# First attention of a two-layer hybrid transformer on one core: the conditioning-vector steps start at item 10, one to every second item, and ScalarE multiplies for the latent stream

## The chip, the cores and the metric

One core of a Trainium2 chip runs the whole program in one launch. The metric is device time in microseconds. TensorE (PE in the rows; PEld is its weight loading), VectorE (DVE), ScalarE (ACT), GpSimd (POOL) and SyncE (SP) each work through a queue of their own in order; the first four compute, SP here starts the DMAs.

## The reference, cut to what matters

Two layers run over 512 latent tokens and 256 context tokens of width 1024; the first uses grouped-query attention, the second latent attention, and each is followed by a squared-ReLU MLP. Every sub-layer is modulated by six vectors (shift, scale, gate, twice) that are linear maps of the conditioning input, one set per stream:

```python
mod_lat = (silu_c @ w_ada[i] + b_ada[i])[:, None, :]
mod_ctx = silu_cc @ w_ada[i] + b_ada[i]
sh_a, sc_a, g_a, sh_m, sc_m, g_m = jnp.split(mod_lat, 6, axis=-1)
...
x = layer_norm(alpha * x + g_a * y_lat, ln_g[i, 0], ln_b[i, 0])
```

In the first attention, latent queries attend in one softmax to 256 context and 512 latent keys, context queries to the context keys alone, with 16 query heads of width 64.

## The kernel before, in words

The first attention works through 8 pairs of heads. A pair has five rounds: first half of the latent queries tile 0, the context round, tile 1, then the two tiles of the second half; 40 rounds in all, here numbered r0 to r39 (r1, r6, r11 ... are context rounds). In a round PE computes the scores of both heads of the pair (lines 852 and 853, for context 843 and 844), DVE takes the negated row maximum (`nm`, line 690; 693 for context), ACT the exponentials (`prob`, line 691; 695 for context). In the next round PE transposes these (line 707), ACT and DVE copy them out (`pT` or `pC`, lines 710 and 712), and later PE multiplies them with the values (line 731), after which `rb` (723), a transpose (740), `rinv` (742) and `o` (743) divide by the row sums. Scores have two buffers (`big`), so the scores of a head wait until the exponentials of the same head in the round before have been read. The query split for the next pair (`QS`, two casts on ACT by line 62, each followed by a subtraction on DVE by line 65) stands in two of the five rounds.

Work that the attention does not need rides along. `fill` is called twice a round, once for each item i (so 80 items), and issues a step of a conditioning vector when its argument is true. There are 32 steps: two vectors (v = 2, 3) in two halves, 8 steps each. A step loads 128x512 of the weight (`araw`, two buffers, a DMA on SP), multiplies it by one column of the conditioning input for each of the two streams (line 204 on POOL or 206 on ACT; stream 0 is the latent one and goes into `atmp`, one buffer; stream 1 overwrites `araw`), and adds both to accumulators on POOL (`aacc`, line 208). The first step of a half writes the accumulators directly. Six items after the eighth step PE sums the accumulators (line 215). At given items the split of the output projection's weights is placed too: `wh` (ACT, line 62, 128x1024) and `wl` (DVE, line 65).

PE's order is written by hand. The order on ACT, DVE, POOL and SP comes from a scheduler that places instructions by its own idea of when they can run, so an instruction may stand far ahead of the place where the program issues it.

Of the kernel before, what the change touches and what calls it, by code (L numbers as in the profile page):

```python
# [39 lines left out]
def backbone(ctx, tc, a, out):  # L40
# [14 lines left out]
    def big():  # L55
        return ps.tile([P, 2, 512], F32, name="big", tag="big", bufs=2)

    def one():
        return ps.tile([P, 512], F32, name="one", tag="one", bufs=4)
# [75 lines left out]
    def vec_bias(layer, v, half, n):  # L135
        w = D // n
        return ada_bias(a["b_ada"][layer, v, half * w : half * w + w].rearrange("(g c) -> g c", g=4), w // 4)

    def ada_finish(layer, v, half, n, o, bias):

        w = D // n
        q = w // 4
        row = ada_row(o[:, 0:q], bias)
        if v % 3 == 2:
            for g in range(4):
                c0 = half * w + g * q
                nc.sync.dma_start(gates[2 * layer + v // 3, :, c0 : c0 + q], row[32 * g : 32 * g + 2, :])
            return
        tp = o[:, 256 : 256 + q]
        m = q // P  # L150
        for c in range(m):
            nc.tensor.transpose(tp[:, c * P : (c + 1) * P], row[:, c * P : (c + 1) * P], ident)
        if (layer, v) not in modT:
            modT[layer, v] = const.tile([P, KD, 2], F32, name=f"modT{layer}{v}")
        mv = modT[layer, v].rearrange("p (n g j) s -> p n j g s", n=n, g=4)
        for s in range(2):
            nc.vector.tensor_copy(
                out=mv[:, half, :, :, s], in_=tp.rearrange("p (c g r) -> p c g r", c=m, g=4)[:, :, :, s]
            )
# [17 lines left out]
    def ada_vec(layer, v, half, n, streams, pools, mult):  # L177

        w = D // n
        rawp, tmpp, accp = pools
        accs, bias = {}, []
        src = a["w_ada"][layer, v]

        def step(k):
            if k == 0:
                bias.append(vec_bias(layer, v, half, n))
            t = rawp(src[k, :, half * w : half * w + w])  # L190
            for s in streams:
                eng = mult(k, s)
                sc = scT[:, k, s : s + 1]
                if k == 0:
                    accs[s] = dst = accp(s)
                elif eng == "dve":
                    nc.vector.scalar_tensor_tensor(
                        out=accs[s], in0=t, scalar=sc, in1=accs[s], op0=ALU.mult, op1=ALU.add
                    )
                    continue  # L200
                else:
                    dst = t if s == streams[-1] else tmpp()
                if eng == "pool":
                    nc.gpsimd.tensor_tensor(out=dst, in0=t, in1=sc.to_broadcast([P, w]), op=ALU.mult)
                else:
                    nc.scalar.activation(dst, t, AF.Identity, scale=sc)  # L206
                if k > 0:
                    nc.gpsimd.tensor_tensor(out=accs[s], in0=accs[s], in1=dst, op=ALU.add)  # L208

        def end():  # L210
            o = one()
            q = w // 4
            for g in range(4):
                for i, s in enumerate(streams):
                    nc.tensor.matmul(
                        o[32 * g : 32 * g + 32, 0:q], onehot[:, 1 - s : 33 - s], accs[s][:, g * q : g * q + q],
                        start=(i == 0), stop=(i == len(streams) - 1),
                    )
            ada_finish(layer, v, half, n, o, bias[0])

        return [lambda k=k: step(k) for k in range(KD - 1)] + [lambda: (step(KD - 1), end)[1]]
# [278 lines left out]
    def ada_raw(src):  # L500
# [4 lines left out]
    ada_pools = (  # L505
        ada_raw, lambda: adp.tile([P, 512], F32, name="atmp", tag="atmp"),
        lambda s: adp.tile([P, 512], F32, name="aacc", tag="aacc", bufs=4),
    )
    phase = ["act"]
    steps = []  # L510
    for v in (2, 3):
        for h in range(2):
            steps += ada_vec(0, v, h, 2, (0, 1), ada_pools, lambda k, s: phase[0])
    fill = Fill(steps, 6)
    qp = pool(st_qkv, "qp")
    rope = raw_tile(a["rope_gqa"].rearrange("p a t d -> p (a t d)"), 512)[:, 0:512]
# [156 lines left out]
    class Attn:  # L673
# [78 lines left out]
        def run(self, first, prep, scores, vcol, o_of, npair, ctx_scores, fill, at):  # L752

            rounds = []
            for p in range(npair):
                rounds += [(p, 0, 0)] + ([(p, None, 0)] if ctx_scores is not None else [])  # L760
                rounds += [(p, 0, 1), (p, 1, 0), (p, 1, 1)]
            state, PT, sums = {0: first}, {}, {}
            av, steps, last = [], [], []
            n = 0

            def score(p, hf, q, h):
                S = big()
                if (p, hf) not in sums:
                    sums[p, hf] = self.ap.tile([P, 2, 2], F32, name="sm", tag="sm", bufs=4)
                if hf is None:  # L770
                    ctx_scores(state[p], h, S)
                    return self.softmax(S, 2, CTX, sums[p, hf][:, :, h])
                scores(state[p], h, NCT + hf * 2 + q, S)
                return self.softmax(S, 1, 384, sums[p, hf][:, q, h : h + 1])

            def turn(p, hf, q, pts):
                if hf is None:
                    PT[p, hf] = t = self.ap.tile([P, 2, NCT, 2, P], F32, name="pC", tag="pC")
                    self.transposed(pts, t.rearrange("p t n h c -> p (t n) h c"), 1)
                    return  # L780
                if q == 0:
                    PT[p, hf] = self.ap.tile([P, 2, NT, 2, P], F32, name="pT", tag="pT", bufs=2)
                self.transposed(pts, PT[p, hf][:, q], self.nact)

            with tc.manual_schedule(engines={nc.tensor.engine}):
                while rounds or last or av:
                    now = []
                    if rounds:
                        p, hf, q = rounds.pop(0)
                        if hf == 0 and q == 0 and p + 1 < npair:  # L790
                            state[p + 1], steps = prep(p + 1)
                        now = [(p, hf, q, [score(p, hf, q, h) for h in range(2)])]
                    ready = av[:1]
                    for it in last:
                        turn(*it)
                    if steps:
                        steps.pop(0)()
                    for f, end in ready:
                        f()
                        if end:  # L800
                            end()
                    av = av[1:]
                    if last and (last[0][1] is None or last[0][2] == 1):
                        p, hf = last[0][:2]
                        lo = 0 if hf is None else NCT + hf * 2
                        av += self.values(
                            PT[p, hf], sums[p, hf],
                            lambda kt, hh, p=p: vcol(kt, 2 * p + hh), range(NCT if hf is None else NT),
                            o_of(p)[:, lo : lo + 2, :],
                        )  # L810
                    last = now
                    for i in (n, n + 1):
                        if fill is not None:
                            fill(i % 5 < 2)
                        for f in at.get(i, []):
                            f()
                    n += 2
                if fill is not None:
                    fill.rest()
# [688 lines left out]
```

## Time and profile before

| | |
|---|---|
| median of 3 runs | 1685.24 us (1681.62 to 1685.29) |
| profiled execution | 1686.92 us, its span 1685.1 us |
| PE busy in the span | 1625.9 us (96%) |
| DVE, ACT, POOL busy | 1117.6, 721.7, 444.0 us |
| first attention | 129 to 332 us of the span |

The profile's span leaves out 1.8 us around it. Busy shares are over the whole program; the stage in question is about an eighth of it.

### The profile page before, as it was taken

The numbers are of one execution on the slowest core, as the hardware profiler recorded it, in microseconds if no ns is written. First come the engines' busy times: TensorE is split into PE (matmuls) and PEld (weight loads), VectorE is DVE, ScalarE is ACT, GpSimd is POOL, SyncE is SP. The second block draws the span as 40 slices with busy tenths as digits, with TensorE's granted clock in tenths as the row PEclk, the third lists the DMA queues.
The fourth block names the chain that finished last, engine by engine and source line by source line (L and its number), as shares of the span: only waits on it lengthen the run. The fifth ranks groups of instructions, "written<-read, shape, count | busy, mean of one in ns | idle before, by whom it ended". The sixth has DMA issues, their size and how long they took to land.

```text
span 1685.1 us, 23746 instructions
## 1 busy us (share of the span) xinstructions
PE 1625.9 (96%) x9266; PEld 1366.8 (81%) x9266; DVE 1117.6 (66%) x1700; ACT 721.7 (43%) x1317; POOL 444.0 (26%) x317
## 2 busy tenths in 40 slices
PE   7998999999999999999999999999999999999996
PEld 6875777778888888898889898888878888888884
DVE  4778888777856667555547666766658655555587
ACT  3324676634643344333112356666653522222221
POOL 0247888034323245223000321000004200000034
PEclk9998999999999999999999999999999999999998
DMA  8413113132434356344213122001022433332222
GB/s 324 137 52 106 51 57 101 58 119 100 164 123 138 105 190 196 123 137 151 75 51 109 61 95 91 1 1 38 26 99 102 164 100 100 100 100 91 97 75 76
DMA packets 51969, 172.05 MB, mean 102 GB/s; under 512 B 6776, under 2 KB 6928, under 8 KB 51856
## 3 DMA queue, kind: packets, MB, share of 16 engines
q1 hardware_dynamic: 51824, 170.51, 30.3%
q8 instruction: 73, 1.20, 0.3%
q14 instruction: 40, 0.33, 0.1%
q10 hardware_dynamic: 32, 0.02, 0.0%
HBM read 161.03 MB, written 9.47 MB: 101 GB/s over the span
## 4 chain that ended last, share of the span: by engine, by line
PE 80%; DVE 10%; ACT 3%; DMA 3%; POOL 2%; issue 2%; DVEq 0%; SPq 0%; ACTq 0%; POOLq 0%
PE one L89 10%; PE one L91 10%; PE one L90 10%; PE big L978 7%; PE big L981 7%; PE big L982 7%; PE one L731 6%; PE one L707 4%; PE one L914 2%; PE one L915 2%; PE one L918 2%; DVE wl L65 2%; POOL xr L208 1%; PE big L1359 1%; PE big L852 1%
## 5 line engine op out<-in xcount | busy, mean ns | idle before, releaser
L62 ACT CAST wh<-raw 128x1024 fp32r<-128x1024 f32 (+3 forms) x172 | 171.9, 1016 | 404.6 <-PE one L91 210.8
L65 DVE TENSOR_TENSOR wl<-raw,wh 128x1024 fp32r<-128x1024 f32 (+3 forms) x172 | 218.6, 1284 | 175.0 <-ACT wh L62 173.8
L978 PE MATMUL big<-actH,wh 128*128 128x384 f32 (+2 forms) x800 | 280.7, 352 | 1.3 <-ACT wh L62 1.3
L981 PE MATMUL big<-actL,wh 128*128 128x384 f32 (+2 forms) x800 | 279.9, 350 | 0.4 <-DVE actL L65 0.3
L982 PE MATMUL big<-actH,wl 128*128 128x384 f32 (+2 forms) x800 | 279.5, 350 | 0.0
L89 PE MATMUL one<-wh,hh 128*128 128x512 f32 x640 | 256.1, 401 | 9.4 <-ACT hh L62 4.4
L91 PE MATMUL one<-wh,hl 128*128 128x512 f32 x640 | 253.9, 398 | 2.8 <-DVE hl L65 2.8
L90 PE MATMUL one<-wl,hh 128*128 128x512 f32 x640 | 255.1, 399 | 1.3 <-DVE wl L65 1.3
L1062 DVE TENSOR_TENSOR yacc<-yacc,one 128x512 f32<-128x512 f32 x260 | 174.4, 682 | 113.5 <-PE one L91 113.2
L208 POOL TENSOR_TENSOR xr<-xr,raw 128x1024 f32<-128x1024 f32 x49 | 129.0, 2633 | 249.2 <-ACT raw L206 247.8
L978 PEld LDWEIGHTS big<-actH,wh 128*128 128x128 f32 x800 | 150.2, 188 | 15.0 <-ACT wh L62 2.1
L981 PEld LDWEIGHTS big<-actL,wh 128*128 128x128 f32 x800 | 150.3, 188 | 13.4 <-DVE actL L65 1.1
L982 PEld LDWEIGHTS big<-actH,wl 128*128 128x128 f32 x800 | 150.1, 188 | 12.6 <-issue 0.4
L89 PEld LDWEIGHTS one<-wh,hh 128*128 128x128 f32 x640 | 121.7, 190 | 41.1 <-ACT hh L62 5.1
L91 PEld LDWEIGHTS one<-wh,hl 128*128 128x128 f32 x640 | 121.2, 189 | 32.0 <-DVE hl L65 3.2
L90 PEld LDWEIGHTS one<-wl,hh 128*128 128x128 f32 x640 | 121.8, 190 | 27.5 <-DVE wl L65 1.7
L691 ACT ACTIVATE prob<-big,nm 128x768 f32<-128x768 f32 x128 | 115.9, 908 | 56.0 <-DVE nm L690 55.8
L690 DVE TENSOR_REDUCE nm<-big 128x1 f32<-128x768 f32 x128 | 119.6, 953 | 14.7 <-PE big L1363 8.6
L707 PE MATMUL one<-ident,prob 128*128 128x128 f32 x832 | 104.1, 274 | 1.7 <-ACT pT L710 1.7
L731 PE MATMUL one<-pT,V 128*64 128x256 f32 x768 | 98.7, 393 | 2.6 <-DVE pT L712 2.6
L707 PEld LDWEIGHTS one<-ident,prob 128*128 128x128 f32 x832 | 95.6, 142 | 5.2 <-ACT pT L710 2.2
L328 POOL TENSOR_TENSOR xr<-xr,ln_g 128x1024 f32<-128x1024 f32 x8 | 20.9, 2617 | 265.4 <-PE one L915 242.8
(246 smaller groups left out, 2844.4 us busy)
## 6 DMA issues: line engine op xcount, KB each, us to landing
raw<-in_mlp_w_dram SPq DMA_DIRECT2D x128, 512.0 KB
raw<-in_w_ada_dram SPq DMA_DIRECT2D x56, 512.0 KB
sraw<-in_w_ada_dram SPq DMA_DIRECT2D x16, 512.0 KB
araw<-in_w_ada_dram SPq DMA_DIRECT2D x32, 256.0 KB
raw<-in_w_o_dram SPq DMA_DIRECT2D x16, 512.0 KB
xr<-xres SPq DMA_DIRECT2D x14, 512.0 KB
raw<-in_w_qkv_dram SPq DMA_DIRECT2D x12, 512.0 KB
ada<-in_w_ada_dram SPq DMA_DIRECT2D x8, 512.0 KB
```

The lines of the kernel that those rows point to most:

```text
L62: return nc.scalar.copy(out=dst, in_=src)
L65: return nc.vector.tensor_tensor(out=dst, in0=src, in1=hi.bitcast(F32), op=ALU.subtract)
L89: nc.tensor.matmul(o, lh, rh, start=start, stop=False)
L90: nc.tensor.matmul(o, lh, rl, start=False, stop=False)
L91: nc.tensor.matmul(o, ll, rh, start=False, stop=stop)
L208: nc.gpsimd.tensor_tensor(out=accs[s], in0=accs[s], in1=dst, op=ALU.add)
L707: nc.tensor.transpose(tp[:, j * P : (j + 1) * P], pts[j % 2][:, k * P : (k + 1) * P], ident)
L731: nc.tensor.matmul(acc[64 * hh : 64 * hh + 64, 0:256], v(kts[n], hh), PT[:, :, n, hh, :], start=(n == 0), stop=(n == len(kts) - 1),)
L978: mm = nc.tensor.matmul(o, wh[:, ks], aH[:, k, s:e], start=(k == 0), stop=False)
L981: nc.tensor.matmul(o, wh[:, ks], aL[:, k, s:e], start=False, stop=False)
L982: nc.tensor.matmul(o, wl[:, ks], aH[:, k, s:e], start=False, stop=(k == KD - 1))
L1062: nc.vector.tensor_tensor(out=yacc[i][:, cs], in0=yacc[i][:, cs], in1=accs[hf], op=ALU.add)
```

## The change

The first product of the two streams moves from POOL to ACT in all 32 steps, and the items at which a step is issued change from two of every five, from item 0 on, to every second one from item 10 on.

```diff
-            steps += ada_vec(0, v, h, 2, (0, 1), ada_pools, lambda k, s: phase[0])
+            steps += ada_vec(0, v, h, 2, (0, 1), ada_pools, lambda k, s: phase[0] if s else "act")
...
-                            fill(i % 5 < 2)
+                            fill(i >= 10 and i % 2 == 0)
```

`phase[0]` is "pool" by the time these steps run. The call of `fill` in the second attention is the same line with other work (`fill` may be None there), and the steps' DMAs, adds and final PE sums are the same in number.

How the change moves instructions is seen in the built programs. First POOL, in the middle of a half, before: one step is the run from one `atmp` product to the next.

```order
L204 TENSOR_TENSOR atmp_1800<-araw_1798,scT_75 128x512
L208 TENSOR_TENSOR aacc_1494<-aacc_1494,araw_1791 128x512
L208 TENSOR_TENSOR aacc_1492<-aacc_1492,atmp_1800 128x512
L204 TENSOR_TENSOR araw_1798<-araw_1798,scT_75 128x512
L204 TENSOR_TENSOR atmp_1908<-araw_1906,scT_75 128x512
L208 TENSOR_TENSOR aacc_1494<-aacc_1494,araw_1798 128x512
```

After, POOL in the first half of a vector, around its third and fourth step:

```order
L208 TENSOR_TENSOR aacc_1766<-aacc_1766,atmp_1880 128x512
L204 TENSOR_TENSOR araw_1878<-araw_1878,scT_75 128x512
L208 TENSOR_TENSOR aacc_1768<-aacc_1768,araw_1878 128x512
L208 TENSOR_TENSOR aacc_1766<-aacc_1766,atmp_1937 128x512
L204 TENSOR_TENSOR araw_1935<-araw_1935,scT_75 128x512
L208 TENSOR_TENSOR aacc_1768<-aacc_1768,araw_1935 128x512
```

Four instructions of a step became three, and the add of `atmp` now waits for ACT; before, the next step's `atmp` product stood ahead of the add that frees `araw`, and now it no longer does.

ACT in round r17 (first the copy `pC` and the exponentials of both heads), before:

```order
L62 CAST QS_2318<-one_2429 64x384 x2
L710 COPY pC_2465<-one_2466 128x512
L691 ACTIVATE prob_2453,sm_2320<-big_2447,nm_2452 128x768
L691 ACTIVATE prob_2462,sm_2320<-big_2456,nm_2461 128x768
L742 COPY rinv_2486<-one_2437 128x256
L723 COPY rb_2536<-sm_2390 128x256
```

The same round of ACT after:

```order
L691 ACTIVATE prob_2439,sm_2291<-big_2433,nm_2438 128x768
L710 COPY pC_2451<-one_2452 128x512
L206 ACTIVATE atmp_2847<-araw_2845,scT_75 128x512
L62 CAST wh_2852<-raw_2658 128x1024
L691 ACTIVATE prob_2448,sm_2291<-big_2442,nm_2447 128x768
L742 COPY rinv_2472<-one_2416 128x256
L206 ACTIVATE atmp_2905<-araw_2903,scT_75 128x512
```

A product and a weight cast now stand between the exponentials of the two heads; this cast stood in round r23 before. The 32 products of line 206 stand on ACT from the stage ahead of the attention (two of them) and from r2 to r29, although the program issues them from r5 to r36.

DVE in the context round r31, before (`nm` of the two heads, a weight split, the copies `pT`):

```order
L693 TENSOR_REDUCE nm_3301<-big_3296 128x2
L65 TENSOR_TENSOR wl_3282<-raw_3095,wh_3281 128x1024
L712 COPY pT_3306<-one_3313 128x512
L65 TENSOR_TENSOR QS_3205<-one_3243,QS_3205 64x384
L712 COPY pT_3306<-one_3319 128x512
```

And after:

```order
L693 TENSOR_REDUCE nm_3291<-big_3285 128x2
L743 TENSOR_TENSOR o5_3087<-one_3195,rinv_3269 128x256
L65 TENSOR_TENSOR wl_3282<-raw_3095,wh_3281 128x1024
L693 TENSOR_REDUCE nm_3301<-big_3296 128x2
L712 COPY pT_3306<-one_3313 128x512
L712 COPY pT_3306<-one_3319 128x512
```

The weight split stands between the two maxima instead of behind both, and the query split no longer stands between the two copies.

## Rows read from the trace of the kernel before

**Rows 1.** The page's first line.

```profile
span 1685.1 us, 23746 instructions
```

**Rows 2.** Windows: busy PE, PEld, DVE, ACT, POOL; granted clock, DMA share, GB/s.

```profile
129.00:168.00 39.00, 31.14 (x219) 22.13 (x218) 32.84 (x60) 18.48 (x43) 30.64 (x26) 0.87 0.28 96
168.00:257.00 89.00, 87.48 (x684) 69.93 (x685) 72.39 (x117) 62.50 (x154) 77.30 (x68) 1.00 0.18 56
281.00:290.00 9.00, 6.53 (x56) 4.44 (x55) 7.67 (x12) 5.53 (x16) 8.84 (x7) 0.83 0.27 80
```

**Rows 3.** Groups of POOL, 129 to 332 us: busy, mean ns, idle before.

```profile
L208 POOL TENSOR_TENSOR aacc<-aacc,araw 128x512 f32<-128x512 f32 x28 | 36.8, 1315 | 0.2
...
L204 POOL TENSOR_TENSOR atmp<-araw,scT 128x512 f32<-128x512 f32 x28 | 29.2, 1043 | 17.4 <-DMA araw<-in_w_ada_dram 17.1 <-POOL araw L204 0.2
```

**Rows 4.** Timeline of POOL in one step: start, us, instruction, idle before.

```profile
169.24 1.28 POOL L208 TENSOR_TENSOR aacc<-aacc,araw 128x512 f32<-128x512 f32 x1
...
173.36 1.04 POOL L204 TENSOR_TENSOR atmp<-araw,scT 128x512 f32<-128x512 f32 x1 [0.61 <-DMA araw<-in_w_ada_dram]
```

**Rows 5.** Groups of ACT, 129 to 332 us.

```profile
L710 ACT COPY pT<-one 128x512 f32<-128x512 f32 x32 | 18.7, 584 | 16.5 <-PE one L707 16.5
...
L62 ACT CAST wh<-raw 128x1024 fp32r<-128x1024 f32 x6 | 6.3, 1052 | 0.0
```

**Rows 6.** Line 206 elsewhere in the program: ns min/median/max.

```profile
L206 ACT ACTIVATE raw<-raw,scT x49: 1144/1153/1157, 433.6 to 792.7; 128x1024 f32<-128x1024 f32 x49
```

**Rows 7.** Timeline of ACT in r17.

```profile
219.37 0.59 ACT L710 COPY pC<-one 128x512 f32<-128x512 f32 x1 [0.51 <-PE one L707]
219.85 0.91 ACT L691 ACTIVATE prob<-big,nm 128x768 f32<-128x768 f32 x1
...
220.74 0.90 ACT L691 ACTIVATE prob<-big,nm 128x768 f32<-128x768 f32 x1
```

**Rows 8.** Timeline of PE: second head's scores of r18.

```profile
222.11 0.34 PE L852 MATMUL big<-KL,QS 128*128 128x384 f32 x1
```

**Rows 9.** Timeline of ACT: the second head's exponentials of r2.

```profile
147.29 0.89 ACT L691 ACTIVATE prob<-big,nm 128x768 f32<-128x768 f32 x1
```

**Rows 10.** Timeline of PE: second head's scores of r3.

```profile
148.32 0.45 PE L852 MATMUL big<-KL,QS 128*128 128x384 f32 x1
```

**Rows 11.** Timeline of ACT in r15 and r16: the query split and rinv.

```profile
212.75 0.47 ACT L62 CAST QS<-one 64x384 fp32r<-64x384 f32 x1 [0.62 <-DVE QS L65]
213.36 0.37 ACT L742 COPY rinv<-one 128x256 f32<-128x256 f32 x1
```

**Rows 12.** Timeline of ACT around r27.

```profile
264.34 0.47 ACT L62 CAST QS<-one 64x384 fp32r<-64x384 f32 x1 [1.37 <-DVE QS L65]
265.85 0.59 ACT L710 COPY pC<-one 128x512 f32<-128x512 f32 x1 [1.03 <-PE one L707]
...
269.94 0.59 ACT L710 COPY pT<-one 128x512 f32<-128x512 f32 x1 [0.47 <-PE one L707]
```

**Rows 13.** Timeline of PE: r5 after its stall, r6, and r31.

```profile
164.01 0.89 PE L610 MATMUL one<-ident,q 128*128 128x128 f32 x3 [2.43 <-ACT pT L710]
164.83 2.81 PE L731 MATMUL one<-pT,V 128*64 128x256 f32 x12
...
174.43 1.52 PE L731 MATMUL one<-pT,V 128*64 128x256 f32 x12
...
286.21 2.15 PE L731 MATMUL one<-pT,V 128*64 128x256 f32 x12 [1.29 <-DVE pT L712]
```

**Rows 14.** Timeline of DVE in r5, r31, and r34.

```profile
160.39 1.20 DVE L252 TENSOR_TENSOR modB<-modA,lnbT 128x16 f32<-128x16 f32 x1
...
283.41 2.15 DVE L65 TENSOR_TENSOR wl<-raw,wh 128x1024 fp32r<-128x1024 f32 x1
...
286.19 0.56 DVE L65 TENSOR_TENSOR QS<-one,QS 64x384 fp32r<-64x384 f32 x1
...
301.15 1.22 DVE L65 TENSOR_TENSOR wl<-raw,wh 128x1024 fp32r<-128x1024 f32 x1
```

## The prediction, on record before the changed kernel ran

> **What bounds the kernel now.** I read the page first, then busy time by stretch, then the groups of ACT and POOL in the attention, then timelines of the rounds in which PE waits. The profiled execution has a span of 1685.1 us [rows 1] and took 1686.92 us in all, 0.1% above the median of 1685.24, so the sum below is made on its span and added to the median. 0.3% of that median is 5.1 us, about what a measurement of this kernel can tell from no change.
>
> The attention has two kinds of stretch [rows 2]. From 168 to 257 us PE is busy 87.48 of 89 us at a granted clock of 1.00: PE is the bound, and ACT with 62.50 us has 26.5 us free, DVE 16.6. From 129 to 168 PE is busy only 31.14 of 39 us, at 0.87, and from 281 to 290 only 6.53 of 9 us, at 0.83. In both, POOL is busy almost throughout (30.64 and 8.84 us). So the change can win in the second kind and lose in the first.
>
> POOL before spends about 1.04 us on a product and 1.32 us on an add of `araw` [rows 3], some 4.7 us a step, and waits 17.4 us for `araw` in all. One turn of its loop shows why: the add that frees `araw` ends at 170.52 (169.24 + 1.28), and the product that waits for the new `araw` starts at 173.36 [rows 4]. That is 2.84 us from a buffer set free to its next use, and the product stands ahead of the next add, so a step took 5.1 us. The steps thus ran from 140 to 298 us, and the old argument of `fill` did not pace them; nor need the new one.
>
> **The change part by part.** It takes 32 products of 1.04 us off POOL, 33 us. A step is then product, two adds: about 3.7 us. That is work on an engine for which PE does not wait in rounds, so it counts only through DVE (below). The DMAs are the same 32.
>
> On ACT it adds 32 products of 128x512. ACT's copies cost 0.584 us at 512 columns and 1.052 at 1024 [rows 5], 0.47 less for half the columns. The trace has line 206 at 128x1024 alone, 1.153 us [rows 6], so I estimate 1.153 - 0.47 = 0.69 us; the bounds are 0.58 (the copy) and 1.15 (the long product). Consecutive instructions overlap: the copy at 219.37 lasts 0.59 us and the next starts at 219.85 [rows 7], so 0.11 comes off, and a product holds the queue for 0.58, say 0.6 us. The total of 19 us fits the idle time of ACT. What matters is where each one stands, because the order moves: a product between the two exponentials of a round delays the second, and with it the second head's scores a round later on PE.
>
> How much room is there? In r17 the second exponentials end at 221.64 (220.74 + 0.90), and the scores that need their buffer start at 222.11 [rows 7, 8]: 0.47 us. In r2 they end at 148.18 [rows 9] and the scores of r3 follow at 148.32 [rows 10], where PE waits for them; so 0.14 of a gap is the least, and the room of a steady round is 0.33 us.
>
> Term 1, r2: a product stands between the two exponentials, where there is no room: +0.6 us. It could be given back if DVE were late in r5 anyway (bounds 0 and 0.6); I take all of it.
>
> Term 2, the query split. In r15 its second cast waits 0.62 us for DVE, and `rinv` follows it [rows 11]. After, `rinv` (0.37 us) stands between the two casts in r6, r11 and r21, in r6 with a product as well. Where `rinv` is ready early it fits the 0.62 us, where its input from PE is late the cast waits for it. I take +0.8 in r6 (product and `rinv` less the overlaps) and +0.4 in each of the others: +1.6 (bounds 0 and 2.4).
>
> Term 3, weight casts between softmaxes. Such a cast holds ACT for 1.052 - 0.11 = 0.94 us, with a product 1.5 us. In r17 both stand ahead of the second exponentials: 1.5 - 0.33 = +1.2. In r21 both stand between the two heads of a context round, which is less pressed; between 0 and 1.2 I take +0.4. In r27 the pair stands behind the cast that ends at 264.81; the copy at 265.85 had waited 1.03 us [rows 12], so it comes 0.5 late, and another product follows before the second exponentials, 0.6 more: with 0.33 of room, +0.8 to +0.9. Together +2.5 (bounds 0.8 and 5).
>
> Term 4, the other products, about 25. Most stand in idle time of ACT: nothing. In r7 and r28 one stands directly ahead of the second exponentials: 0.6 - 0.33 each, +0.5. In r28 there is a wait too. A buffer comes round in product, add, product, add and DMA: 0.7 + 1.28 + 1.04 + 1.32 + 2.84 = 7.2 us. The product in r27 starts at 264.8, so the one two steps later can't start before 272, and its place, behind the copy at 269.94 [rows 12], is 270.5 plus what r27 was delayed, 271.4. ACT then stands still for 0.6 us with the exponentials behind it. Together with a little for the rest, +1.5. Bounds: 0, if every one is covered, and 15 (25 x 0.6), if none is; nearer the low end, since ACT is free for 30% of that stretch.
>
> Term 5, the clock. After the stalls in r5 and r31 the twelve value products take 2.81 and 2.15 us against 1.52 in r6 [rows 13]; the granted clock in those stretches was 0.87 and 0.83 [rows 2], between the levels of 1.2 and 2.4 GHz. A new stall of 1.2 us, as in r17, may cost 0 to 1.3 us so; I take +1.0 for all.
>
> Term 6, what comes back in r31. There the weight split on DVE takes 2.15 us, against 1.22 in r34, when POOL is done [rows 14]; behind it the copies come late, PE waits 1.29 us, and runs its products 0.63 slower. After, POOL should be done by about 275 us, since the products on ACT stand up to r29, and the query split (0.56 us) no longer stands between the copies. That is 0.93 + 0.56 = 1.5 us earlier, more than the 1.29. I take 1.29 + 0.63 and 0.3 for the sums of line 215 behind: -2.2 (bounds -0.9 and -4). But the split now stands ahead of the second head's maximum, which is why not more.
>
> The stall of r5 (2.43 us of waiting, and 1.29 of slower products) I leave as it is: the two small instructions on DVE there, one of them 1.20 us for 128x16, are held by POOL, and POOL is still at work there, since its steps begin at 140 us as before.
>
> Sum: 0.6 + 1.6 + 2.5 + 1.5 + 1.0 - 2.2 = +5.0 us, 1690 us.
>
> **A rule that speaks for a gain.** DVE's weight split took 2.15 us beside POOL and 1.22 without it [rows 14]. The Trainium skill, "SBUF — State Buffer", section "Who interferes with whom", says that a DVE instruction with two inputs in SBUF and a GpSimd instruction that reads SBUF shut each other out for the whole instruction; the trace agrees, with 0.93 us. By that rule 32 fewer POOL products leave DVE more freedom everywhere, and the first rival follows.
>
> **The rivals.**
> Faster: POOL's lighter load decides. Were POOL idle when DVE's two instructions come in r5, the 2.43 + 1.29 = 3.7 us of r5 would go, with 4 at most in r31: -7.7. With 0.8 of term 3's low bound and 1.5 for terms 1, 2 and 4 that leaves -5.4, about 1680. It decides if PE's wait in r5 falls below 1 us. For it: PE lost 7.9 of 39 us in the first stretch, with POOL busy 79% of it. Against: POOL's first steps still fall there. Chance 0.19.
>
> Same: PE is the bound, ACT's idle 26.5 us take the 13 us of products that fall in that stretch, the order's inversions meet early inputs (term 2 at 0, terms 3 and 4 near their low bounds, +1.5 together), and r31 gives 2.2 back: +0 to +1, about 1685. Chance 0.21.
>
> Much slower: ACT's queue stands still. ACT now waits for `araw` and for `atmp` (one buffer), in order. If steps need 5.1 us as before, while their places on ACT come every 4.2 us (32 from 142 to 275), each product waits up to 0.9 us there; half of that on PE in 25 of them is 11 us, with further clock losses as in term 5: about 1699. It decides if ACT waits for DMA or POOL in more than ten products. Against: the add that frees `araw` no longer stands behind the next product. Chance 0.18.
>
> That the steps do not begin five rounds later is certain from the order and is in every case.
>
> **Numbers.** My case (+2 to +9, 1687 to 1694) is the likeliest at 0.42. Its middle lies at the 0.3% bound, 1690.3, but I have counted only the stalls that I could see in the order, so I put two thirds of it above: 0.28. Slower by over 0.3% is that and the worst case, 0.46; the same is the second rival and the rest of mine, 0.35; faster 0.19. The range runs from the first rival, 1680, to 1701, just past the worst case.
>
> **What would show it.** Right: second scores on PE waiting about 1.2 us for ACT in r18, about 0.8 in r28, in r31 1.22 us for the weight split and no wait of 1.29 us for the copy, POOL done before 280 us, line 206 at 0.69 us. Wrong: r5's wait gone (faster), or many idle times of ACT that end with `araw` or `aacc` ahead of line 206 (slower by more).

## The result, and the profile after

The changed kernel takes 1693.36 us (median; 1693.17 to 1693.74) against 1684.43 before: a ratio of 1.0051 with a 95% interval of 1.0033 to 1.0068, so slower by 0.5%, 8.6 us by the ratio. The forecast was 1690 us, slower, within 1680 to 1701.

The groups of ACT and POOL in the attention (129 to 342 us) of the changed kernel, with busy us, mean ns, idle time before and what ended it; the POOL rows answer to [rows 3]:

```profile
L206 ACT ACTIVATE atmp<-araw,scT 128x512 f32<-128x512 f32 x27 | 19.6, 726 | 3.3 <-DMA araw<-in_w_ada_dram 2.8 <-POOL aacc L208 0.4
...
L62 ACT CAST wh<-raw 128x1024 fp32r<-128x1024 f32 x6 | 6.2, 1042 | 1.5 <-DMA raw<-in_w_o_dram 1.5
```

```profile
L208 POOL TENSOR_TENSOR aacc<-aacc,atmp 128x512 f32<-128x512 f32 x28 | 36.9, 1319 | 25.4 <-ACT atmp L206 25.3
L208 POOL TENSOR_TENSOR aacc<-aacc,araw 128x512 f32<-128x512 f32 x28 | 36.7, 1311 | 1.8
```

A product on ACT takes 0.726 us (0.69 was estimated). POOL no longer waits for DMA but for ACT, 25.3 us: it is paced by the places that the products have there. ACT itself waits 2.8 us for `araw` at the head of its queue, and two weight casts wait 1.5 us for their own DMA, with the exponentials behind them.

The stretches from 129 to 281 us, the first two with the same bounds as in [rows 2] (busy PE, PEld, DVE, ACT, POOL, then granted clock, DMA share and GB/s):

```profile
129.00:168.00 39.00, 29.00 (x215) 21.89 (x216) 32.76 (x60) 20.67 (x47) 27.18 (x22) 0.91 0.30 101
168.00:257.00 89.00, 85.10 (x638) 65.86 (x635) 67.11 (x110) 72.14 (x168) 60.26 (x53) 0.98 0.17 54
257.00:281.00 24.00, 21.46 (x149) 15.89 (x149) 18.89 (x29) 18.57 (x42) 17.14 (x14) 0.93 0.31 99
```

ACT is busier by 10 us in the middle stretch, as it should be, and still has 17 of 89 us free; yet PE is busy 2.4 us less. So ACT's total is not enough to explain the loss. From the start of the first scores of a round (lines 852 and 843 in PE's timeline) to those of a later one, in us:

| | before | after | difference |
|---|---|---|---|
| r0 to r6 | 38.54 | 39.42 | +0.88 |
| r6 to r16 | 45.27 | 48.24 | +2.97 |
| r16 to r31 | 68.10 | 75.31 | +7.21 |
| r31 to r32 | 8.84 | 6.55 | -2.29 |
| r32 to r39 | 29.32 | 29.59 | +0.27 |
| r0 to r39 | 190.08 | 199.11 | +9.03 |

The whole of the loss arises in the attention; the two spans differ by 6.7 us, since the rest of the program took 2.3 us less in this pair of profiles. How one part of it arises shows ACT's timeline of r17 and r18 after, which answers to [rows 7]:

```profile
223.63 0.90 ACT L691 ACTIVATE prob<-big,nm 128x768 f32<-128x768 f32 x1 [0.68 <-DVE nm L690]
224.52 0.57 ACT L710 COPY pC<-one 128x512 f32<-128x512 f32 x1
224.99 0.73 ACT L206 ACTIVATE atmp<-araw,scT 128x512 f32<-128x512 f32 x1
225.61 1.05 ACT L62 CAST wh<-raw 128x1024 fp32r<-128x1024 f32 x1
226.55 0.91 ACT L691 ACTIVATE prob<-big,nm 128x768 f32<-128x768 f32 x1
```

And PE there, which answers to [rows 8]:

```profile
226.36 0.33 PE L853 MATMUL big<-KH,QS 128*128 128x384 f32 x1
227.60 0.45 PE L852 MATMUL big<-KL,QS 128*128 128x384 f32 x1 [0.91 <-ACT prob L691]
```

The second exponentials end at 227.46 and the scores start 0.14 us later, the same least gap as in r2 before [rows 9, 10]: PE is held by ACT here, and the second head's scores follow the first's 1.85 us later (225.75 in the same timeline) in place of 0.78.

### The profile page after: what moved, and what is told of

Read it like the earlier page. It is cut to its first block, busy times and chain, and to the rows that moved or that the text cites. A ratio compares the mean times of both kernels' runs of the same rounds, so it can differ in the third digit from the quotient of the medians.

```text
span 1691.8 us, 23728 instructions
## 1 busy us (share of the span) xinstructions
PE 1625.5 (96%) x9266; PEld 1364.3 (81%) x9266; DVE 1117.4 (66%) x1700; ACT 741.3 (44%) x1349; POOL 412.4 (24%) x285
## 4 chain that ended last, share of the span: by engine, by line
PE 75%; DVE 11%; ACT 5%; DMA 4%; POOL 3%; issue 2%; DVEq 0%; SPq 0%; ACTq 0%; POOLq 0%
PE one L89 9%; PE one L90 9%; PE one L91 9%; PE big L978 7%; PE big L982 7%; PE big L981 7%; PE one L731 5%; PE one L707 3%; DVE wl L65 2%; PE one L914 2%; PE one L918 2%; PE one L915 2%; POOL xr L208 2%; DMA raw<-in_w_ada_dram 1%; DVE xr L197 1%
## 5 line engine op out<-in xcount | busy, mean ns | idle before, releaser
L65 DVE TENSOR_TENSOR wl<-raw,wh 128x1024 fp32r<-128x1024 f32 (+3 forms) x172 | 223.9, 1315 | 174.8 <-ACT wh L62 173.5
```

The costliest lines, as they stand in the source:

```text
L65: return nc.vector.tensor_tensor(out=dst, in0=src, in1=hi.bitcast(F32), op=ALU.subtract)
```

## The experiments

The runs are called e1 to e3 and e5 to e10 (none is called e4). The edits of e1 and e2 are shown against the kernel before, those of e3 and e5 against the changed kernel, and those of e6 to e10 against e3; all are cut to the lines that change. Three explanations were set against each other. **Place** (mine): the scheduler put the products, and weight casts with them, between exponentials for which PE waits. **Times** (rival A): the new times of the steps cost. **Load** (rival B): 19 us more on ACT cost wherever they stand. The chip's own median of the kernel before lay between 1683.75 and 1685.2 us, and each ratio is against runs on the same chip. "Attention" is r0 to r39 as in the table above (190.08 before, 199.11 after), from one profiled execution of each kernel; where that execution lies far from the median of its kernel, its time is given.

**The products alone (e1).**

```diff
-    lambda k, s: phase[0])
+    lambda k, s: phase[0] if s else "act")
...
     fill(i % 5 < 2)
```

> The products of the latent stream on ScalarE, the old times of the steps. My theory (the loss is the place of the products, and of the weight casts that stand right behind them, between the exponentials of a round): ScalarE's order is nearly that of the changed kernel, so 1690 to 1695 us. Rival A (the loss comes from the steps' new times): 1682 to 1687.

1695.43 us, 0.4 above my range, ratio 1.0063 (1.0052 to 1.0075); attention 201.33 us. The products alone bring the whole loss.

**The times alone (e2).**

```diff
-    fill(i % 5 < 2)
+    fill(i >= 10 and i % 2 == 0)
```

> The new times of the steps, all products on GpSimd. My theory: GpSimd runs its steps as soon as the data is there, whatever the items say, so 1682 to 1687 us, as before. Rival A: 1690 or more.

1683.03 us, ratio 0.9999 (0.9986 to 1.0011); attention 189.18 us. Rival A falls: with all products on GpSimd the new times neither cost nor give anything in sum. POOL's first product for these steps starts at 141.47 us, at 140.41 before.

**The products held at their place in the program (e3).** The scheduler is told not to move them ahead. The weight casts, which carry the same mark already and by the built order stand behind what precedes them in the program, are then back at r23 and later (in the trace they run in r24, r26, r29, r31, r34 and r36, as before).

```diff
-    nc.scalar.activation(dst, t, AF.Identity, scale=sc)
+    ins = nc.scalar.activation(dst, t, AF.Identity, scale=sc)
+    if hold[0]:
+        tc.keep_in_program_order(ins)
```

`hold[0]` is true during the first attention alone; this and the other runs with a hold have four lines more, so line 206 is 208 in them, POOL's 204 and 208 are 206 and 212, 250 is 254, 610 is 614, 690 is 694, 710 is 714 and 731 is 735.

> The changed kernel with ScalarE's products held at the place where the program issues them, at the end of rounds r5 to r36; the weight casts are then back in r23 to r35. My theory: most of the loss goes, 1682 to 1688 us. Rival B (19 us more work on ScalarE costs wherever it stands): 1691 or more.

1679.32 us, ratio 0.9969 (0.9957 to 0.9981): below my range, faster than the kernel before by 0.3%, and 13.8 us (0.82%) better than the changed one, with the same work on the same engines. Attention 183.68 us. Rival B falls. ACT in this run, 129 to 335 us:

```profile
L208 ACT ACTIVATE atmp<-araw,scT 128x512 f32<-128x512 f32 x28 | 20.5, 730 | 0.0
```

Not one of these products waits for anything. Of the 15.4 us of attention between the changed kernel and this one, 9.9 lie in r6 to r31 and 6.2 in r0 to r6. The gain against before lies in r0 to r6 (33.25 against 38.54) and r31 (6.68 against 8.84). In r5 DVE computes two small instructions for the modulation. Before, the first one and POOL's two adds beside it were (the second, 1.20 us from 160.39, is in [rows 14]):

```profile
159.18 1.18 DVE L250 TENSOR_SCALAR modA<-modT 128x16 f32<-128x16 f32 x1
...
159.04 1.29 POOL L208 TENSOR_TENSOR aacc<-aacc,araw 128x512 f32<-128x512 f32 x1
160.29 1.27 POOL L208 TENSOR_TENSOR aacc<-aacc,atmp 128x512 f32<-128x512 f32 x1
```

Each of the two on DVE ends 0.03 us after the add on POOL beside it (160.36 after 160.33, 161.59 after 161.56). In e3 they read in DVE's timeline:

```profile
156.89 0.18 DVE L254 TENSOR_SCALAR modA<-modT 128x16 f32<-128x16 f32 x1
157.10 0.18 DVE L256 TENSOR_TENSOR modB<-modA,lnbT 128x16 f32<-128x16 f32 x1
157.31 0.96 DVE L694 TENSOR_REDUCE nm<-big 128x1 f32<-128x768 f32 x1
```

POOL there is idle, since its first add waits for the first held product:

```profile
139.88 1.22 POOL L206 TENSOR_TENSOR aacc<-araw,scT 128x512 f32<-128x512 f32 x1
166.12 1.28 POOL L212 TENSOR_TENSOR aacc<-aacc,atmp 128x512 f32<-128x512 f32 x1 [25.01 <-ACT atmp L208]
```

And PE's wait of 2.43 us with its slow products behind [rows 13] has become this:

```profile
159.83 0.55 PE L614 MATMUL one<-ident,q 128*128 128x128 f32 x3 [0.54 <-ACT pT L714]
160.30 1.52 PE L735 MATMUL one<-pT,V 128*64 128x256 f32 x12
```

**Casts apart from the products (e5).** The two blocks of the loop are exchanged, so that a cast follows other work than a step. In the built program the casts then no longer move ahead with the products: they run in pairs in r24, r29 and r34.

```diff
-    if fill is not None:
-        fill(i >= 10 and i % 2 == 0)
     for f in at.get(i, []):
         f()
+    if fill is not None:
+        fill(i >= 10 and i % 2 == 0)
```

> The changed kernel with the weight casts issued ahead of the step of their item, so that a cast no longer stands right behind a product that was moved ahead; the products stay where they are. My theory: the pair of product and cast in r17, r21 and r27 cost about 2.5 us, so 1690 to 1692 us. If casts don't matter: 1693.4.

1692.54 us, ratio 1.0049 (1.0036 to 1.0061): inconclusive in time, its interval covers the changed kernel's ratio. In the trace the attention takes 195.70 us, 3.4 less than after, and r18 lasts 4.33 us from scores to scores instead of 5.27 after (4.09 before): the cast in r17 cost its 0.94 us on ACT in full. How much all casts cost stays open, between next to nothing (the two ratios) and about 3 us (the two traces): the profiled execution of e5 took 1690.26 us, 2.3 below the median, that of the changed kernel 1693.74, 0.4 above. Most of the loss is there without the casts in any case.

**Held, at the old times (e6).**

```diff
-    fill(i >= 10 and i % 2 == 0)
+    fill(i % 5 < 2)
```

> The products held at the place where the program issues them, as in e3_products_held, but at the old times, two of every five items from item 0. If the 5 us that e3 won in r2 to r5 came from GpSimd standing idle there (the later start): they go back, 1683 to 1687 us. If they came from fewer products on GpSimd alone: 1678 to 1681.

1682.15 us, ratio 0.9981 (0.9972 to 0.9991); attention 187.55 us. It lies between e3 and before, in neither of the two ranges. Of the 5.3 us that e3 won from r0 to r6, 3.7 are gone (36.90), all in r1 to r3; r5 wins its 3.52 us here as in e3, since POOL waits for a held product and is idle in r5 here too (from 158.2 to 166.5 us). The rest of the attention is within 0.2 us of e3's in sum. So once the products stay in place, the later start is worth 3.9 us of these traces, or 2 us (0.12%) by the two ratios, whose intervals overlap at their ends. Against e1, which has the same old times, the hold is worth 0.82% as well (1.0063 and 0.9981), and POOL starts its steps equally early in both (139.4 and 139.5 us): so it is not the late start of POOL that makes the difference.

**Nearly all on GpSimd, but started late (e7).**

```diff
-    lambda k, s: phase[0] if s else "act")
+    lambda k, s: phase[0] if k else "act")
```

> The new times, with the two products of the first step of each half held on ScalarE and all others on GpSimd, so that GpSimd can't begin before r5 but has nearly all the work. The later start gives the 5 us of r2 to r5 back here too; but a step takes 5.1 us on GpSimd and a round 4.2 to 4.5, so it ends some 15 us late, and PE waits at the end of the attention for the sums: 1684 to 1695 us. If the later start gives nothing: 1690 to 1700.

1679.48 us, below my range, ratio 0.9971 (0.9957 to 0.9985); attention 183.54 us. The gain of r0 to r6 came as expected (33.11), the stall at the end did not: GpSimd ended at 308 us, in time. I had taken 5.1 us a step from the loop of the kernel before; the groups of POOL in this run, 129 to 345 us:

```profile
L212 POOL TENSOR_TENSOR aacc<-aacc,atmp 128x512 f32<-128x512 f32 x28 | 35.8, 1278 | 21.4 <-ACT aacc L208 20.9
L206 POOL TENSOR_TENSOR atmp<-araw,scT 128x512 f32<-128x512 f32 x28 | 31.3, 1119 | 14.7 <-DMA araw<-in_w_ada_dram 14.7
```

It waits less for DMA (14.7 us against 17.4), and a step takes about 4.6 us (162 to 308 us for 32). So this kernel needs no product on ACT at all beyond the eight that hold the start.

**Both streams on ACT, held (e8).**

```diff
-    lambda k, s: phase[0] if s else "act")
+    lambda k, s: "act")
```

> As e3_products_held, but the products of both streams on ScalarE, 64 of 0.6 us, held at the end of the rounds. If only the place counts: 1678 to 1684 us. If ScalarE's time counts (it is busy 82% of the middle stretch in e3 and would be at about 95%): 1687 to 1700.

1683.32 us, ratio 0.9991 (0.998 to 1.0002); attention 188.68 us. This lies in the range for the place alone. ACT is busy 83.00 of 89 us in the middle stretch, and in the trace the 5 us that the early rounds win are mostly lost later (71.58 us from r16 to r31 against 67.99 in e3); but the profiled execution took 1687.48 us, 4.2 above the median. Load may begin to tell, and if so only at twice what the change puts there.

**One vector ahead, the other held (e9 and e10).** The hold is given to one of the two vectors.

```diff
-    if hold[0]:
+    if hold[0] and v == 3:
```

> The changed kernel with the products of the second vector (v = 3) held at the place of the program, those of the first vector left ahead as the change has them. If the loss adds up place by place: in the changed kernel the rounds up to r15 lost 3 us against before and the rounds after them 6, so 1681 to 1687 us, with the loss of r2 to r15 there and none after (r31 gives back 2).

1685.78 us, ratio 1.0008 (0.9998 to 1.0018); attention 191.60 us. r0 to r16 take 87.14 us, as after (87.66), r16 to r31 take 67.75, as in e3 (67.99). The profiled execution took 1689.82 us, 4.0 above the median.

```diff
-    if hold[0]:
+    if hold[0] and v == 2:
```

> The other half: products of the first vector held, those of the second vector ahead. Adding up by place: r2 to r15 win 5 to 6 us as in e3_products_held, and the rounds from r16 on lose 4 to 8 against it, so 1682 to 1688 us. If the loss were not additive but came of having any product ahead: both halves near 1690.

1687.68 us, ratio 1.0015 (1.0004 to 1.0026); attention 197.42 us. r0 to r16 take 78.96 us, as in e3 (78.92), r16 to r31 79.03, worse than after (75.31). The profiled execution took 1692.41 us, 4.7 above the median. Against e3 the two halves lose 0.39% and 0.46%, together 0.85%, and the change as a whole loses 0.82%: by the ratios the loss adds up. By the traces it does so for the first vector alone; in attention time the halves lose 7.9 and 13.7 us against e3, together 21.7, the change 15.4. So each vector's loss falls in its own rounds, but that it is the same loss as in the changed kernel is shown for the first one only. In e10 ACT waits for data in front of the products (the view of line 208, the last row being idle us of its engine, and times):

```profile
L208 ACT ACTIVATE atmp<-araw,scT x28: 712/727/738, 165.6 to 296.2; 128x512 f32<-128x512 f32 x28
...
  DMA araw<-in_w_ada_dram: 9.5, 9
```

9.5 us in 9 waits is the rival "ACT's queue stands still" in a kernel near the changed one, where it was 2.8 us.

## Why the prediction was right, and where its sum fell short

The direction and its cause held: with the products back at their place in the program the loss is gone (e3, and e6 against e1), the new times alone cost nothing (e2), and one vector ahead brings its loss back in the rounds where it stands (e9, e10). The hold also takes back what moved along with the products, the weight casts on ACT and the place of their splits in DVE's rounds; of these the casts are parted from the products in e5 alone.

The sum of +5.0 was short of the 9.0 us of the two traces' attention (8.6 by the ratio). Terms 2 and 5 were sized too small, and one step was missing: the new times move PE's sums of line 215 into other rounds, for which the prediction had nothing. By its terms (a product or cast in one round shows in the scores of the next):

- Term 1, r2: as forecast. The second scores of r3 start 1.49 us after the first, 0.88 before; that is 0.61, with 0.6 forecast, and they start 0.14 us after the exponentials that stand behind the product (148.65 + 0.89). The whole of r0 to r6 lost 0.88, but not for this reason alone: r2 and r3 lost 1.45 and 2.11 us, and r1 and r5 gave 1.23 and 1.46 back. In r3 the clock adds 1.29: after a wait of 3.49 us (1.27 before) PE runs at a granted clock of 0.50, which is the level of 1.2 GHz, and the twelve transposes take 2.76 us against 1.47 in r4 of the same trace. Such shifts are in the run with the new times alone too (r3 +1.23, r5 -1.65, -0.44 in sum). ACT and PE after:

```profile
148.04 0.71 ACT L206 ACTIVATE atmp<-araw,scT 128x512 f32<-128x512 f32 x1
148.65 0.89 ACT L691 ACTIVATE prob<-big,nm 128x768 f32<-128x768 f32 x1
...
148.19 0.69 PE L852 MATMUL big<-KL,QS 128*128 128x384 f32 x1 [3.49 <-ACT prob L691]
...
149.68 0.69 PE L852 MATMUL big<-KL,QS 128*128 128x384 f32 x1
```

- Term 2, the query split: r6 lost 1.48 (0.8 forecast). r11 lost 0.47 (0.4); the sums of line 215 left that round, worth 0.60 in the run with the times alone, so the true price was about 1.1. r21 gained 0.41, and 0.60 in the run with the times alone. So the term was 1.6, and the runs show 1.5 + 1.1 + 0.2 = 2.8.
- The sums that left r11 and r21 stand in r15 and r23, which lost 0.76 and 0.77; r25 lost 0.69. So much they lost in e3 too (0.77, 0.86, 0.69), where no product stands badly, and nothing in e6 with the old times, so that is not the products'; what costs in r25, where no sum stands, is open. In e2 and e3 r26 makes up for it (-1.90, -1.84), in the changed kernel it does not.
- Term 3: r17's pair cost 1.18 in r18 (1.2 forecast), r21's 0.60 in r22 (0.4), and r27's 0.65 in r28 (0.8 to 0.9), where PE waits 0.39 us for the second exponentials: 2.4 against 2.5.
- Term 4 came to nearly its size (1.8 against 1.5), but in part by luck, from causes that it did not have. The product in r7 cost 0.24 in r8 (0.27). The wait on `araw` that I had worked out from the buffer's round (7.2 us) came one round earlier than I put it, in r27, 1.23 us long instead of 0.6; behind it stands the pair of term 3, so the two cannot be parted, and they cost 0.65 together. The product in r28 cost the second scores of r29 nothing (0.79 us behind the first, 0.78 before). But r29 and r30 lost 0.85 and 0.73, and I had nothing for them. I had priced three of the casts that moved. Two of the others moved from r30 and r35 to r25 and r30, and came before their own data. ACT's timeline after:

```profile
261.07 1.05 ACT L62 CAST wh<-raw 128x1024 fp32r<-128x1024 f32 x1 [0.74 <-DMA raw<-in_w_o_dram]
...
273.80 0.72 ACT L206 ACTIVATE atmp<-araw,scT 128x512 f32<-128x512 f32 x1 [1.23 <-DMA araw<-in_w_ada_dram]
...
288.72 1.05 ACT L62 CAST wh<-raw 128x1024 fp32r<-128x1024 f32 x1 [0.79 <-DMA raw<-in_w_o_dram]
```

The wait of 0.79 us stands ahead of exponentials of r30. In r29 it is DVE that is late, with the split that belongs to a cast: it stands ahead of the first row maximum of the round, where it stood behind both before, and takes 2.05 us beside POOL (1.21 before). PE waits 0.76 us for the exponentials that need this maximum. In r26, too, a split of 1.88 us now stands between the two maxima and ahead of the query split. DVE after, and PE at the start of r30:

```profile
266.89 1.88 DVE L65 TENSOR_TENSOR wl<-raw,wh 128x1024 fp32r<-128x1024 f32 x1
...
283.10 2.05 DVE L65 TENSOR_TENSOR wl<-raw,wh 128x1024 fp32r<-128x1024 f32 x1
285.07 1.81 DVE L690 TENSOR_REDUCE nm<-big 128x1 f32<-128x768 f32 x2
...
287.10 0.44 PE L852 MATMUL big<-KL,QS 128*128 128x384 f32 x1 [0.76 <-ACT prob L691]
```

- Term 5, the clock: +1.0 forecast for all, and r26 and r27 show 1.6. In r26 PE waits 0.85 us for a copy and then 0.93 for the query split, and runs its products at a lower clock, 2.65 us against 1.52; from 270.01 to 272.66 us the granted clock is 0.54, near the level of 1.2 GHz. The first scores of r27 are still slow (0.69 us against 0.44 before), which is r27's loss of 0.48. Of r26's loss of 1.35, 1.13 are the slow products; against e3, where PE does not wait in r26, it is 3.19, the largest of any round. PE's timeline after:

```profile
268.54 0.55 PE L610 MATMUL one<-ident,q 128*128 128x128 f32 x3 [0.85 <-ACT pT L710]
270.01 2.65 PE L731 MATMUL one<-pT,V 128*64 128x256 f32 x12 [0.93 <-DVE QS L65]
...
272.59 0.69 PE L852 MATMUL big<-KL,QS 128*128 128x384 f32 x1
```

In r17 and r18, where I had expected it, the value products take 1.08 to 1.52 us, as ever, and the granted clock is 1.00: a wait of 0.91 us cost nothing more there. Nor is it the second wait: in e2 PE waits 0.75 and 0.96 us in r31, and the twelve products behind take 1.52. I can't say from these rows what decides it.

- Term 6, r31: -2.29 against -2.2. The weight split took 1.22 us, as forecast, and the wait of 1.29 us for the copy is gone; PE now waits 0.43 for a copy ahead of the sums. DVE's timeline after:

```profile
295.15 1.22 DVE L65 TENSOR_TENSOR wl<-raw,wh 128x1024 fp32r<-128x1024 f32 x1
```

POOL ended at 290 us, not 275 or 280: it was paced by ACT, whose rounds had slipped by 11 us. It was done ahead of the split all the same. But that was not what the gain hung on. In e3 POOL works until 309 us and the split in r31 takes 1.89, and the round still gains 2.15; in e7, with a split of 1.52 us ahead of both copies as after, it gains 2.54. In e2, with DVE's order of before and a split of 1.83 us, it gains 0.47. So the 0.93 us of the faster split were not needed for the gain. What after, e3 and e7 have in common and e2 lacks is that no query split stands between the two copies; no run tries that alone.

Of the signs named ahead, PE's wait in r18 was 0.91 us (about 1.2), in r28 0.39 (about 0.8), and a product took 0.726 us (0.69); POOL was not done before 280 us. The signs of a wrong forecast did not show: r5's wait was still 2.01 us.

The first rival, the one of the Trainium skill's rule on shared ports ("SBUF — State Buffer", "Who interferes with whom"), was not what this change did: in r5 DVE's two instructions still took 0.98 and 0.96 us, because POOL was at work there, as I had said. But its mechanism is real, and e3 shows it with its price: with POOL idle, 1.20 us became 0.18, and r5 lasts 3.52 us less, over half of the 6.4 us that e3's attention gains on before. The five traces in which POOL is idle there (e3, e6, e7, e8, e10) have 0.17 to 0.18 us for both instructions and the same 3.52 or 3.53 us; the six others have 0.72 to 1.20. That is the rule's two-input case (`modB`); `modA`, with one input in SBUF, went from 1.18 to 0.18 as well, which the same section allows for a `tensor_scalar` in its two-port mode; no run here tells in which mode it ran.

## What to carry to other kernels

Work that is moved to an engine with free time is not free there: ask between which two instructions it will stand, and whether another engine waits for the second. Where a scheduler sets the order, read the built order before arguing from the numbers in the source; here the five rounds by which the steps were to begin later existed only once the products were held in place, and then the same change won 0.3% where it had lost 0.5%. When an instruction moves ahead, look also for what is pinned behind it, whether that one's data will be there, and what becomes of the order on the other engines.

## What the runs showed of the hardware that I had not expected

A `tensor_scalar` of DVE on 128x16 values took 1.18 us beside a busy GpSimd, 0.98 in the changed kernel, and 0.18 with GpSimd idle. Beside a busy GpSimd it ended 0.03 us after the 128x512 instruction there, so its time was set by the end of its neighbour. Two waits of PE in one round (0.85 and 0.93 us in r26 of the changed kernel, 0.75 and 0.96 in r31 of e2) were followed by twelve value products of 2.65 us at a granted clock of 0.54 in the one case and of 1.52 us at 1.00 in the other.
